# High and low part of the input in one product of 512 columns, both sums added at eviction

## The chip, the cores and the metric

The kernel runs on one core of a Trainium2 chip. The metric is the device time of one execution in microseconds, the median of several runs. TensorE (PE) multiplies, PEld is its weight load, VectorE is DVE, ScalarE is ACT, GpSimd is POOL, SyncE is SP. TensorE's clock is granted at one of two levels, 1.2 and 2.4 GHz; the profile gives it as a share of the higher.

## What is computed

Two transformer blocks, one behind the other, on 256 tokens of width 2048, all in fp32. Cut to the parts around the change:

```python
# first block, feed-forward (FFN_HIDDEN = 5632)
h = rms_norm(x, ln_ffn_pre)
u = causal_depthwise_conv(h @ w_ffn_up, ffn_conv_w, ffn_conv_b)     # 2048 -> 2 * 5632, 3 taps
gate, up = jnp.split(u, [FFN_HIDDEN], axis=-1)
f = (gelu_tanh(gate) * up) @ w_ffn_down                             # 5632 -> 2048
x = x + rms_norm(f, ln_ffn_post)

# second block, after its mixer: peer_ffn, 8 heads, 16 experts of 16384 for each head and token
q = (hf @ w_pq).reshape(T, 8, 2, 128)                               # routing queries
s = einsum('thpc,hpnc->thpn', q, sub_keys)                          # then top 16 of 128, twice, and of their sums
act = gelu(einsum('cd,ckd->ck', h, take(u_tab, experts))) * gate    # first table
out = einsum('ck,ckd->cd', act, take(v_tab, experts))               # second table
```

Ahead of the feed-forward the first block has an attention and a state-space mixer, and the second block has a recurrent mixer and an attention ahead of its experts.

## The kernel before

**Precision by two parts.** Every large product is made in the type fp32r from a high and a low part: for weights w = hi + lo and input x = xh + xl the kernel sums hi·xh, hi·xl and lo·xh in PSUM. The input's parts are made once (`k.hh`, `k.hl`, each 128 x 16 blocks x 256 tokens; in the feed-forward's second product `gh`, `gl`, 44 blocks). The weights' parts are made as they stream in: `_stream` (L232 on) loads `raw` from memory on SP's queue, ScalarE copies it to `hi` (L252), VectorE makes `lo = raw - hi` (L255). In the first block a chunk of hi and lo is 1024 columns (four blocks of 128 input rows by 256 output columns) with three buffers, in the second 512 columns (two blocks) with four.

**A step.** `_proj` takes the blocks of one group of 256 output columns: for each block and each half of 128 output columns it issues three matmuls of 256 columns (tokens), each with weights of its own, into one PSUM bank `acc`. A step over 16 blocks is 16 x 2 x 3 = 96 matmuls, one over 44 blocks 264. The weights are the stationary side, the input is the moving side. All matmuls are recorded at L260.

**Feed-forward** (`_ffn`, L684). 44 steps over `w_up`, the first three of them held open together and fed in parts (`_lead`, `LEAD2`) while the input's blocks arrive. Behind each step VectorE multiplies `acc` by the token's factor into `u` (L700), does the three taps of the convolution (L704, L707), ScalarE the gelu (L709), and the result is split into `gh` and `gl` (L710 to L712). Then eight steps over `w_dn`, each evicted by ScalarE (squares, L633 and L636) and VectorE (scaling, L626).

**Routing and first table** (`_peer`, L1485 on; `_Route.head`, L1353). 64 steps over the first table `u`; before every third of the first 24 a head is computed: a step over `w_pq`, its eviction to `pq` (L1359), eight small products with the sub-keys into `ps_sk`, then the top values on VectorE. Step i of the table gives two columns of experts for all tokens. Up to step 27 (`done == 0`) it is evicted straight to its place (L1568) and put through the gelu. From step 27 on `spread` builds two tokens' selection from one-hot products (`ps_g`), which ScalarE and VectorE take out of PSUM (L1542, L1543), and the steps from 28 are evicted to `gtmp` (L1573). `acc` has three buffers of one bank in all these places; PSUM has eight banks.

**Second table.** Products of 512 columns into `o` (hi·ah, lo·ah, hi·al), each with weights of its own, beside gathered rows from memory.

The order of instructions on each engine comes from a planner that simulates the kernel's timeline with estimated durations and priorities; each engine then works its list in order.

## Time and profile before

| | |
|---|---|
| median of three runs | 3312.84 us (3309.78 to 3317.23) |
| the profiled execution's own time | 3315.16 us |
| its span, first to last instruction | 3313.4 us |
| mean granted TensorE clock | 0.989 |
| matmuls | 24762 |
| busy: PE, PEld, DVE, ACT, POOL | 97%, 91%, 77%, 49%, 33% of the span |

A row's duration on PE runs from a matmul's start to its modelled end and overlaps the next ones, so matmuls are priced by the distance between starts. "Idle before" is the time in which the engine stood still ahead of an instruction, with what ended it. A row of the windows view gives the stretch and its length, then for each engine the busy time and in brackets the instructions that touch the stretch.

### The profile page before, as it was taken

Reading aid. Unit: us, or ns where it says so; the run is one execution under the profiler, and the core shown is the slowest. Engines: PE = TensorE matmul, PEld = TensorE weight load, DVE = VectorE, ACT = ScalarE, POOL = GpSimd, SP = SyncE. Lnnn points to the kernel's source line nnn. Section 1 sums busy time; section 2 is a strip of 40 time slices with the busy share of each in tenths; the row PEclk is TensorE's granted clock in tenths of the full one; section 3 lists DMA queues with packets and bytes.
Section 4 is the critical chain, followed back from the end, with each engine's and each line's share of the span. In section 5 each row is a group of like instructions: output and inputs, shape, how many; then the busy total and the mean of one; then the engine's idle time right before and its main releaser. Section 6 shows DMA issues by size and latency. Waiting matters only on the chain.

```text
span 3313.4 us, 66459 instructions
## 1 busy us (share of the span) xinstructions
PE 3217.2 (97%) x24762; PEld 3024.0 (91%) x24762; DVE 2556.5 (77%) x6016; ACT 1614.8 (49%) x3131; POOL 1079.8 (33%) x1266
## 2 busy tenths in 40 slices
PE   8999999999999989999999899999999999999998
PEld 8999899999999979888868899999999997777776
DVE  8775587777754468788875587877999997898998
ACT  4444354444433345455554544445556554555554
POOL 2110100000000034444430000003889976666663
PEclk9999999999999989999999999999999999999999
DMA  5445445555555546543417776666666669999996
GB/s 198 160 162 172 151 159 179 186 183 182 187 179 185 182 158 223 157 144 122 127 44 251 245 226 201 194 194 202 191 183 197 187 196 339 353 344 347 346 346 234
DMA packets 240372, 680.50 MB, mean 205 GB/s; under 512 B 59184, under 2 KB 89776, under 8 KB 215856
## 3 DMA queue, kind: packets, MB, share of 16 engines
q1 hardware_dynamic: 168848, 560.53, 51.9%
q0 software_dynamic: 20480, 83.90, 7.1%
q10 hardware_dynamic: 50720, 31.82, 3.3%
q8 instruction: 194, 3.18, 0.4%
q14 instruction: 130, 1.06, 0.1%
HBM read 649.55 MB, written 60.16 MB: 214 GB/s over the span
## 4 chain that ended last, share of the span: by engine, by line
PE 83%; DVE 8%; DMA 5%; ACT 2%; issue 1%; POOL 1%; ACTq 0%; SPq 0%; DVEq 0%
PE acc L260 57%; PE o L260 15%; PE held L260 3%; DVE lo L255 2%; DMA raw<-in_w_out 1%; PE R L260 1%; PE ps_g L260 1%; ACT hi L252 1%; DVE hl L350 1%; PE ps_S L260 1%; DVE ltmp L1040 1%; DMA x3n<-nat 1%; PE ps_p L260 0%; DMA dst<-s 0%; PE ps_sc L260 0%
## 5 line engine op out<-in xcount | busy, mean ns | idle before, releaser
L252 ACT ACTIVATE hi<-raw 128x512 fp32r<-128x512 f32 (+1 forms) x1582 | 1145.3, 731 | 1223.3 <-PE acc L260 740.6
L255 DVE TENSOR_TENSOR lo<-raw,hi 128x512 fp32r<-128x512 f32 (+1 forms) x1492 | 1227.5, 835 | 555.8 <-ACT hi L252 550.8
L260 PE MATMUL acc<-hh,hi 128*128 128x256 f32 x4928 | 1401.4, 285 | 13.0 <-ACT hh L349 11.6
L260 PE MATMUL acc<-hh,lo 128*128 128x256 f32 x4928 | 1401.9, 285 | 11.4 <-DVE lo L255 10.4
L260 PE MATMUL acc<-hl,hi 128*128 128x256 f32 x4928 | 1399.0, 284 | 6.1 <-DVE hl L350 5.9
L260 PEld LDWEIGHTS acc<-hh,hi 128*128 128x128 f32 x4928 | 934.8, 190 | 16.5 <-ACT hh L349 12.3
L260 PEld LDWEIGHTS acc<-hh,lo 128*128 128x128 f32 x4928 | 931.3, 189 | 16.8 <-DVE lo L255 13.3
L260 PEld LDWEIGHTS acc<-hl,hi 128*128 128x128 f32 x4928 | 936.6, 190 | 9.7 <-DVE hl L350 8.5
L260 PE MATMUL o<-lo,ah 128*128 128x512 f32 x768 | 305.0, 397 | 2.1 <-DVE lo L255 2.0
L260 PE MATMUL o<-hi,al 128*128 128x512 f32 x768 | 303.8, 396 | 0.0
L1456 POOL DMA_INDIRECT vrow<-wide,prow x256 | 261.1, 1020 | 66.7 <-issue 40.8
L1525 POOL TENSOR_SCALAR oh<-iota,sel 128x128 fp32r<-128x128 f32 x256 | 203.0, 803 | 93.2 <-PE ps_g L260 79.7
L260 PE MATMUL o<-hi,ah 128*128 128x512 f32 x768 | 221.9, 398 | 8.5 <-ACT hi L252 7.6
L699 POOL MEMSET u<- 128x4 f32 x44 | 4.5, 103 | 653.5 <-DVE y L707 510.3
L260 PE MATMUL acc<-gh,lo 128*128 128x256 f32 x704 | 199.2, 283 | 0.0
L260 PE MATMUL acc<-gl,hi 128*128 128x256 f32 x704 | 199.2, 283 | 0.0
L260 PE MATMUL acc<-gh,hi 128*128 128x256 f32 x704 | 199.2, 283 | 0.0
L255 POOL TENSOR_TENSOR lo<-raw,hi 128x512 fp32r<-128x512 f32 (+1 forms) x90 | 133.3, 1482 | 166.1 <-ACT hi L252 156.0
L260 PEld LDWEIGHTS o<-hi,ah 128*128 128x128 f32 x768 | 143.2, 188 | 48.2 <-ACT hi L252 13.5
L260 PEld LDWEIGHTS o<-lo,ah 128*128 128x128 f32 x768 | 144.5, 188 | 40.0 <-DVE lo L255 5.1
L1478 DVE SCALAR_TENSOR_TENSOR o<-vrow,pval,o 128x512 f32<-128x512 f32 x254 | 179.0, 750 | 0.0
L260 PEld LDWEIGHTS o<-hi,al 128*128 128x128 f32 x768 | 144.6, 188 | 35.0 <-POOL al L1603 0.2
(480 smaller groups left out, 4675.5 us busy)
## 6 DMA issues: line engine op xcount, KB each, us to landing
raw<-in_u SPq DMA_DIRECT2D x256, 512.0 KB, 4.6
raw<-in_w_up SPq DMA_DIRECT2D x85, 1024.0 KB, 5.2
raw<-in_v SPq DMA_DIRECT2D x128, 512.0 KB, 6.3
raw<-in_w_in SPq DMA_DIRECT2D x43, 1024.0 KB, 5.2
raw<-in_w_dn SPq DMA_DIRECT2D x40, 1024.0 KB, 4.8
wide<-in_vs SPq DMA_DIRECT2D x128, 256.0 KB, 4.8
raw<-in_v SPq DMA_DIRECT2D x128, 256.0 KB, 6.0
raw<-in_w_rkv SPq DMA_DIRECT2D x48, 512.0 KB, 3.9
```

Source lines behind the costliest of these rows:

```text
L252: nc.scalar.activation(hi[:, :m], raw[:, a:a + m], AF.Copy)
L255: k.low = eng.tensor_tensor(lo[:, :m], raw[:, a:a + m], hi[:, :m].bitcast(F32), op=OP.subtract)
L260: return k.nc.tensor.matmul(out, lhsT, rhs, start=start, stop=stop, skip_group_check=True)
L350: k.nc.vector.scalar_tensor_tensor(lo, t, scale, hi.bitcast(F32), op0=OP.mult, op1=OP.subtract)
L699: nc.gpsimd.memset(u[:, :, 0:2], 0.0)
L1040: nc.vector.tensor_tensor(tmp[:, :, 0:t], tt[:, :, 0:t], lq[:, 0:t, t][:, None, :].to_broadcast([128, 8, t]), op=OP.mult)
L1456: nc.gpsimd.indirect_dma_start(r, None, wide, bass.IndirectOffsetOnAxis(ap=picks.row[:, t, j:j + 1], axis=0), element_offset=128 * t)
L1478: i = nc.vector.scalar_tensor_tensor(acc[t], v, w, acc[t], op0=OP.mult, op1=OP.add)
L1525: nc.gpsimd.tensor_scalar(a[:, j], iota, sel[:, 0, t:t + 1], None, op0=OP.is_equal)
```

## The change

A new helper `_proj2` does a step with two matmuls for each block and half instead of three: hi times [xh | xl], 512 columns into a whole bank, and lo times xh, 256 columns added to the bank's first half. So a step's result has two banks, one for each half of the output columns. `_sum2` takes it out: ScalarE copies the second halves of both banks (the sum of hi·xl) to SBUF, VectorE adds the first halves. For this the input's two parts lie side by side in one tile (`hx`, `gx`). It is used in all 44 steps over `w_up`, in seven of the eight over `w_dn`, in the eight heads and in table steps 0 to 27; the other steps keep `_proj` and write the first bank of their two. `acc` has three such tiles in the feed-forward (with two instead of three for `psw`) and two in routing and tables.

```diff
@@ -260,6 +260,27 @@
     return k.nc.tensor.matmul(out, lhsT, rhs, start=start, stop=stop, skip_group_check=True)
 
 
+def _proj2(k, ps, w, kts, x, first=True, last=True):
+    k0, k1 = kts
+    kt = k0
+    for hi, lo, m in _stream(k, w[:, k0 * 256:k1 * 256], (k1 - k0) * 256):
+        for a in range(0, m, 256):
+            for c in range(2):
+                cs = slice(a + c * 128, a + c * 128 + 128)
+                _mm(k, ps[:, c].rearrange("p n t -> p (n t)"), hi[:, cs], x[:, kt].rearrange("p n t -> p (n t)"),
+                    start=first and kt == k0)
+                _mm(k, ps[:, c, 0], lo[:, cs], x[:, kt, 0], stop=last and kt == k1 - 1)
+            kt += 1
+def _sum2(k, out, ps):
+    k.nc.scalar.activation(out, ps[:, :, 1], AF.Copy)
+    k.nc.vector.tensor_tensor(out, ps[:, :, 0], out, op=OP.add)
 def _proj(k, ps, w, kts, xh, xl, first=True, last=True, natural=False):
 
     k0, k1 = kts
@@ -287,12 +308,16 @@
             kt += 1
 
 
-def _lead(k, w, prs, parts, name="acc"):
-
-    held = [k.acc.tile([128, 2, 256], F32, name=name) for _ in prs]
+def _lead(k, w, prs, parts, name="acc", both=False):
+    held = [k.acc.tile([128, 2, 2, 256] if both else [128, 2, 256], F32, name=name) for _ in prs]
     for n, part in enumerate(parts):
         for ps, pr in zip(held, prs):
-            _proj(k, ps, w[pr], part, k.hh, k.hl, first=n == 0, last=n == len(parts) - 1)
+            ends = dict(first=n == 0, last=n == len(parts) - 1)
+            if both:
+                _proj2(k, ps, w[pr], part, k.hx, **ends)
+            else:
+                _proj(k, ps, w[pr], part, k.hh, k.hl, **ends)
     return held
 
 
@@ -684,20 +709,22 @@
 def _ffn(k, I, c2, sqa):
     nc, tc = k.nc, k.tc
     g1 = c2.enter_context(tc.tile_pool(name="g1", bufs=1))
-    gh = g1.tile([128, 44, 256], F32R, name="gh")
-    gl = g1.tile([128, 44, 256], F32R, name="gl")
+    gx = g1.tile([128, 44, 2, 256], F32R, name="gx")
+    gh, gl = gx[:, :, 0], gx[:, :, 1]
     _, rb = _token_rstd(k, [sqa[:, 0], sqa[:, 1]], D, g1, "c")
     with tc.tile_pool(name="g2", bufs=2) as g2:
-        lead = _lead(k, I["w_up"], range(3), LEAD2)
+        lead = _lead(k, I["w_up"], range(3), LEAD2, both=True)
         for j in range(44):
             if j < 3:
                 ps = lead[j]
             else:
-                ps = k.acc.tile([128, 2, 256], F32, name="acc")
-                _proj(k, ps, I["w_up"][j], (0, KT), k.hh, k.hl)
+                ps = k.acc.tile([128, 2, 2, 256], F32, name="acc")
+                _proj2(k, ps, I["w_up"][j], (0, KT), k.hx)
+            z = g2.tile([128, 2, 256], F32, name="z")
+            _sum2(k, z, ps)
             u = g2.tile([128, 2, 258], F32, name="u")
             nc.gpsimd.memset(u[:, :, 0:2], 0.0)
-            nc.vector.tensor_tensor(u[:, :, 2:258], ps, _bc2(rb), op=OP.mult)
+            nc.vector.tensor_tensor(u[:, :, 2:258], z, _bc2(rb), op=OP.mult)
             y = g2.tile([128, 2, 256], F32, name="y")
             for n in range(2):
                 t = j + 44 * n
@@ -714,10 +741,16 @@
         f = g3.tile([128, KT, 256], F32, name="f2")
         sqs = [sqa]
         for pr in range(8):
-            ps = k.acc.tile([128, 2, 256], F32, name="acc")
-            _proj(k, ps, I["w_dn"][pr], (0, 44), gh, gl)
-            _sq_acc(k, g3, sqs, ps, pr)
-            _scaled(k, f, ps, "ln_ffn_post", pr)
+            ps = k.acc.tile([128, 2, 2, 256], F32, name="acc")
+            if pr < 7:
+                z = f[:, pr * 2:pr * 2 + 2]
+                _proj2(k, ps, I["w_dn"][pr], (0, 44), gx)
+                _sum2(k, z, ps)
+            else:
+                z = ps[:, 0]
+                _proj(k, z, I["w_dn"][pr], (0, 44), gh, gl)
+            _sq_acc(k, g3, sqs, z, pr)
+            _scaled(k, f, z, "ln_ffn_post", pr)
         _, rb = _token_rstd(k, _sq_list(sqs), D, g3, "d")
         _residual(k, g4, f, rb, "norm1", sqa)
 
@@ -1353,10 +1386,11 @@
     def head(self, h):
         k, p2 = self.k, self.p2
         nc = k.nc
-        ps = k.acc.tile([128, 2, 256], F32, name="acc")
-        _proj(k, ps, self.I["w_pq"][h], (0, KT), k.hh, k.hl)
+        ps = k.acc.tile([128, 2, 2, 256], F32, name="acc")
+        _proj2(k, ps, self.I["w_pq"][h], (0, KT), k.hx)
         q = p2.tile([128, 2, 256], F32, name="pq")
-        nc.vector.tensor_tensor(q, ps, _bc2(self.rb), op=OP.mult)
+        _sum2(k, q, ps)
+        nc.vector.tensor_tensor(q, q, _bc2(self.rb), op=OP.mult)
         sp = k.psw.tile([128, 2, 2, 128], F32, name="ps_sk", tag="psw")
         i0 = None
         for t in range(2):
@@ -1506,7 +1540,7 @@
 
     with ExitStack() as sctx:
         with ExitStack() as c:
-            k.acc = c.enter_context(tc.tile_pool(name="accp", bufs=3, space=bass.MemoryType.PSUM, side="right"))
+            k.acc = c.enter_context(tc.tile_pool(name="accp", bufs=2, space=bass.MemoryType.PSUM, side="right"))
             k.psw = c.enter_context(tc.tile_pool(name="pswp", bufs=4, space=bass.MemoryType.PSUM))
             t2 = tctx.enter_context(tc.tile_pool(name="rt2", bufs=2))
             route = _Route(k, I, rb, t1, t2)
@@ -1561,16 +1595,18 @@
                     gate = g1.tile([128, 256], F32, name="gate")
                     nc.scalar.activation(gate.bitcast(F32R), sel[:, 2], AF.Copy)
                     nc.vector.tensor_tensor(sel[:, 2], sel[:, 2], gate, op=OP.subtract)
-                ps = k.acc.tile([128, 2, 256], F32, name="acc")
-                _proj(k, ps, I["u"][i], (0, KT), k.hh, k.hl)
+                ps = k.acc.tile([128, 2, 2, 256], F32, name="acc")
                 dst = next(parts(2 * i, 2 * i + 2))[0]
                 if done == 0:
-                    nc.vector.tensor_tensor(dst, ps, _bc2(rb), op=OP.mult)
+                    _proj2(k, ps, I["u"][i], (0, KT), k.hx)
+                    _sum2(k, dst, ps)
+                    nc.vector.tensor_tensor(dst, dst, _bc2(rb), op=OP.mult)
                     nc.scalar.activation(dst, dst, AF.Gelu)
                     keep(dst, i, 0, 256)
                 else:
+                    _proj(k, ps[:, 0], I["u"][i], (0, KT), k.hh, k.hl)
                     tmp = g1.tile([128, 2, 256], F32, name="gtmp")
-                    nc.vector.tensor_tensor(tmp, ps, _bc2(rb), op=OP.mult)
+                    nc.vector.tensor_tensor(tmp, ps[:, 0], _bc2(rb), op=OP.mult)
                     nc.scalar.activation(tmp[:, :, :done], tmp[:, :, :done], AF.Gelu)
                     keep(tmp, i, 0, done)
                     if done < 256:
@@ -1649,8 +1685,8 @@
 def _first_block(k, I, xp, sqa):
     nc, tc = k.nc, k.tc
     with ExitStack() as c1:
-        k.psw = c1.enter_context(tc.tile_pool(name="psw", bufs=3, space=bass.MemoryType.PSUM))
         with ExitStack() as c2:
+            k.psw = c2.enter_context(tc.tile_pool(name="psw", bufs=3, space=bass.MemoryType.PSUM))
             mp = c2.enter_context(tc.tile_pool(name="mix", bufs=1))
             mh = mp.tile([128, KT, 256], F32R, name="mh")
             ml = mp.tile([128, KT, 256], F32R, name="ml")
@@ -1675,6 +1711,7 @@
             with tc.tile_pool(name="rsd", bufs=3) as rp:
                 _residual(k, rp, f, rb, "ln_ffn_pre", sqa)
         with ExitStack() as c2:
+            k.psw = c2.enter_context(tc.tile_pool(name="pswf", bufs=2, space=bass.MemoryType.PSUM))
             k.acc = c2.enter_context(tc.tile_pool(name="accf", bufs=3, space=bass.MemoryType.PSUM))
             _ffn(k, I, c2, sqa)
 
@@ -1761,8 +1798,8 @@
     nc.vector.memset(k.ones, 1.0)
     hctx, cctx = ExitStack(), ExitStack()
     hp = hctx.enter_context(tc.tile_pool(name="h", bufs=1, side="right"))
-    k.hh = hp.tile([128, KT, 256], F32R, name="hh")
-    k.hl = hp.tile([128, KT, 256], F32R, name="hl")
+    k.hx = hp.tile([128, KT, 2, 256], F32R, name="hx")
+    k.hh, k.hl = k.hx[:, :, 0], k.hx[:, :, 1]
     cp = cctx.enter_context(tc.tile_pool(name="cols", bufs=1, side="right"))
     k.cols = cp.tile([128, I["cols"].shape[1]], F32, name="cols")
     sqa = cp.tile([128, 2, 256], F32, name="sqa")
```

## Rows read from the trace of the kernel before

**Rows 1.** The page: busy time, granted clock, chain that ended last

```profile
PE 3217.2 (97%) x24762; PEld 3024.0 (91%) x24762; DVE 2556.5 (77%) x6016; ACT 1614.8 (49%) x3131; POOL 1079.8 (33%) x1266
...
PEclk9999999999999989999999999999999999999999
...
PE 83%; DVE 8%; DMA 5%; ACT 2%; issue 1%; POOL 1%; ACTq 0%; SPq 0%; DVEq 0%
PE acc L260 57%; PE o L260 15%; PE held L260 3%; DVE lo L255 2%; DMA raw<-in_w_out 1%; PE R L260 1%; PE ps_g L260 1%; ACT hi L252 1%; DVE hl L350 1%; PE ps_S L260 1%; DVE ltmp L1040 1%; DMA x3n<-nat 1%; PE ps_p L260 0%; DMA dst<-s 0%; PE ps_sc L260 0%
```

**Rows 2.** Windows: busy of PE, PEld, DVE, ACT, POOL; clock, DMA share, GB/s

```profile
400.00:450.00 50.00, 40.16 (x298) 38.75 (x297) 38.78 (x86) 24.18 (x45) 0.00 (x0) 0.86 0.41 137
500.00:900.00 400.00, 400.00 (x3336) 400.00 (x3335) 292.09 (x453) 172.29 (x208) 3.50 (x34) 1.00 0.56 184
950.00:1150.00 200.00, 200.00 (x1669) 200.00 (x1668) 88.97 (x81) 76.67 (x76) 9.24 (x5) 1.00 0.54 185
1200.00:1700.00 500.00, 471.80 (x4347) 427.07 (x4347) 411.85 (x1136) 256.36 (x628) 237.70 (x327) 0.97 0.47 146
1850.00:1905.00 55.00, 47.16 (x357) 44.84 (x356) 33.40 (x63) 30.46 (x58) 8.22 (x6) 0.94 0.69 216
1910.00:2240.00 330.00, 330.00 (x2757) 330.00 (x2756) 264.33 (x753) 157.24 (x255) 0.00 (x0) 1.00 0.65 203
2300.00:2700.00 400.00, 398.38 (x3328) 397.97 (x3327) 382.50 (x1225) 237.26 (x673) 346.85 (x386) 1.00 0.65 190
2750.00:3250.00 500.00, 491.03 (x2079) 389.38 (x2078) 448.14 (x1066) 252.65 (x463) 341.64 (x363) 1.00 0.97 349
```

**Rows 3.** The page's costliest groups: busy us, mean ns, idle before

```profile
L260 PE MATMUL acc<-gh,hi 128*128 128x256 f32 x704 | 199.2, 283 | 0.0
```

**Rows 4.** Timeline of DVE: start, us, instruction, idle before; two table evictions

```profile
2273.97 0.69 DVE L1568 TENSOR_TENSOR sa<-acc,rs_bcp 128x512 f32<-128x512 f32 x1 [0.20 <-PE acc L260]
...
2285.49 0.69 DVE L1568 TENSOR_TENSOR sb<-acc,rs_bcp 128x512 f32<-128x512 f32 x1 [0.16 <-PE acc L260]
```

**Rows 5.** Windows of tile o alone: PE, PEld, DVE; clock, DMA share

```profile
2900.00:2950.00 50.00, 50.00 (x215) 40.20 (x214) 16.93 (x24) 1.00 0.96 336
```

**Rows 6.** Timeline of PE: products with w_dt's 16-column weights

```profile
58.82 0.28 PE L260 MATMUL ps_dt<-hh,wdh 128*16 128x256 f32 x1
...
59.95 0.28 PE L260 MATMUL ps_dt<-hl,wdh 128*16 128x256 f32 x1
```

**Rows 7.** Groups by form: squares (950:1150), u (500:900), selection out of PSUM (2300:2700)

```profile
L636 ACT ACTIVATE sqp<-acc 128x512 f32<-128x512 f32 x5 | 2.9, 582 | 0.0
...
L700 DVE TENSOR_TENSOR u<-acc,rs_bcc 128x512 f32<-128x512 f32 x35 | 24.2, 692 | 21.9 <-PE acc L260 21.9
...
L1542 ACT ACTIVATE gsum<-ps_g 128x104 f32<-128x104 f32 x122 | 30.6, 251 | 18.7 <-DVE sa L1545 11.9 <-DVE sb L1545 2.1 <-DVE sb L1543 1.4
L1543 DVE TENSOR_TENSOR gsum<-ps_g,gsum 128x104 f32<-128x104 f32 x121 | 30.5, 253 | 0.0
```

**Rows 8.** Timeline of ACT and DVE at a step's boundary of the first product

```profile
700.05 1.06 ACT L252 ACTIVATE hi<-raw 128x1024 fp32r<-128x1024 f32 x1 [1.81 <-PE acc L260]
...
700.86 0.73 DVE L704 TENSOR_SCALAR y<-u,cols 128x256 f32<-128x256 f32 x2
701.50 1.22 DVE L255 TENSOR_TENSOR lo<-raw,hi 128x1024 fp32r<-128x1024 f32 x1
702.64 0.48 DVE L707 SCALAR_TENSOR_TENSOR y<-u,cols,y 128x256 f32<-128x256 f32 x1
```

**Rows 9.** Timeline of DVE and PE: a head's query and its products

```profile
2025.96 0.69 DVE L1359 TENSOR_TENSOR pq<-acc,rs_bcp 128x512 f32<-128x512 f32 x1 [0.20 <-PE acc L260]
...
2029.01 0.50 PE L260 MATMUL ps_sk<-sk,pq 128*128 128x128 f32 x3
```

**Rows 10.** Timeline of PE and DVE: a late step's last matmul, its eviction

```profile
2707.35 0.28 PE L260 MATMUL acc<-hh,lo 128*128 128x256 f32 x1
...
2714.90 0.68 DVE L1573 TENSOR_TENSOR gtmp<-acc,rs_bcp 128x512 f32<-128x512 f32 x1
```

## Prediction

> **What bounds the kernel now.** I read the page first. TensorE is busy for 97% of the span at full clock nearly throughout, and the chain of work that ended last is 83% TensorE, 57% of it products into the tile acc [rows 1]. A high busy share alone doesn't prove a bound, since matmuls overlap, so I cut the span into stages with the windows view [rows 2]. In the feed-forward's first product (500 to 900 us), its second (950 to 1150), the routing with the early table steps (1910 to 2240) and the late table steps (2300 to 2700) TensorE has no idle time to speak of, while VectorE is at 73%, 44%, 80% and 96%, ScalarE at 38% to 59% and the DMA engines at 54% to 66%. So in the first three of these, which the change touches, time is the number of matmuls times their pitch. Two short stretches are different: the start of the feed-forward (400 to 450 us, TensorE 40.2 of 50 and a mean granted clock of 0.86, thus partly at the lower of its two levels) and the start of the routing (1850 to 1905, 47.2 of 55). There the matmuls wait for their inputs.
>
> **The pitch now.** The duration of a matmul row (283 ns, [rows 3]) overlaps its neighbours and is no price. The price is start to start. In the window from 950 to 1150 us 1669 matmuls of 256 columns touch 200 us; about two lie in it only partly, so 200 / 1667 = 120.0 ns. Two evictions of neighbouring early table steps confirm it: 2285.49 - 2273.97 = 11.52 us for 96 matmuls, again 120.0 ns [rows 4].
>
> **The change, part by part.** (1) For each block of 128 input rows and 128 output columns (a "pair" of old and new form below) three matmuls of 256 columns, each with its weight load, become one of 512 and one of 256. The columns streamed stay 768; what goes is one matmul and one weight load. What a 512-column product of the same types costs is shown by the second table's products into o: 215 touch 50 us without idle time, each lasts about 0.39 us, so 1.7 lie in it only partly and 50 / 213.3 = 234.4 ns [rows 5]. I take this value, since the row has the same types, the same 128-column weights, a load for each product and no wait. A pair then goes from 3 x 120.0 = 360.0 to 234.4 + 120.0 = 354.4 ns, a gain of 5.6 ns; the bounds, 226.7 and 240 ns for the 512 columns, are the first two rivals below. What that gain consists of is seen from w_dt's products: 256 columns with weights of only 16 columns go at (59.95 - 58.82) / 10 = 113 ns [rows 6]. A full weight load thus seems to cost about 7 ns a product, and the rest grows with the columns: 2 x 113 + 7 = 233, near the 234.4 seen.
>
> How many pairs: first product 44 x 16 x 2 = 1408; second, seven of eight, 7 x 44 x 2 = 616; queries 8 x 16 x 2 = 256; table steps 0 to 27 (the code's done is still zero there) 28 x 16 x 2 = 896. Sum 3176. From these I take off the 96 pairs of the feed-forward's three held tiles and 96 at the start of the routing, where the input sets the pace [rows 2]; 3080 - 96 = 2984 remain, times 5.6 ns = **16.7 us** less. (With all of them, 17.8.)
>
> (2) The eviction grows. Each of 44 + 7 + 8 + 28 = 87 steps gets a ScalarE copy of 128x512 out of PSUM (0.582 us by the nearest row, the squares out of acc) and a VectorE add with one side in PSUM (0.692 us, like u's eviction) [rows 7]. That is 51 us of ScalarE and 60 us of VectorE in all; in the first product VectorE goes from 73% to 79%, at most 86% in the early table steps. I cost it at nothing: the matmuls of the next step write another acc tile meanwhile, and a step lasts 11.5 us against 1.3 us more eviction. If that cover were gone everywhere, it would cost 87 x 1.27 = 111 us; a gain isn't possible, as nothing is removed from these engines. What waits behind it: on ScalarE the next high-part copy, on VectorE the next low part. At a step's boundary near 700 us the copy for three chunks ahead starts at 700.05 and its low part ends at 702.72; two chunks of 24 matmuls (5.8 us) are ready before it is wanted, near 705.8 [rows 8]. So 3.1 us of cover stand against 1.3.
>
> (3) In the eight heads TensorE's products with the sub-keys wait for the query. The query is there at 2026.65 and they start at 2029.01, 2.36 us later [rows 9], so 1.27 us more costs nothing; without the cover it would be 8 x 1.27 = 10 us.
>
> (4) acc in routing and table steps has two buffers instead of three, each of two banks. With two, step n+2 waits for the eviction of step n. In the late steps, where VectorE is fullest, the latest eviction I found starts at 2714.90, 7.5 us after its step's last matmul at 2707.35, and the next step lasts over 11.5 us [rows 10]. About 4 us of cover are left: nothing. If it were gone, each late microsecond would be one of TensorE.
>
> (5) Both parts of the input in one tile, psw opened with two buffers for the feed-forward, the first 512-column product wanting the low part one matmul earlier: 0.12 us once at each start, no more. The last of the second product's steps keeps the old form, so the path into the norm behind it is the old one. No DMA is added or moved; the loads of later weights only come as early as TensorE frees their buffers, at 54% to 66% DMA share.
>
> (6) The order on each engine is planned from estimated times, so stages with idle gaps (1200 to 1700 us, TensorE 471.8 of 500 [rows 2]) may come out a little differently though their code is the same. I bound this at 5 us either way, about a sixth of these gaps.
>
> **Sum.** The profiled execution took 3315.16 us (span 3313.4), 2.3 above the median of 3312.84. 3315.2 - 16.7 = 3298.5 for it, and on the median 3312.8 - 16.7 = **3296 us**, 0.5% faster; its own range by (6) and the excluded pairs is 3289 to 3306.
>
> **Rivals.** *A fixed cost for each matmul.* At the granted 2.4 GHz 256 columns take 106.7 ns, so 13.3 ns of the 120.0 are something else. If that is fixed, 512 columns take 213.3 + 13.3 = 226.7, the pair gains 13.3 ns and the time is 3312.8 - 39.7 = 3273. For it: the one place with 512 columns is also the one where DMA engines are at 97% [rows 2], which might slow it there. Against it: the 234.4 itself. The Trainium skill (TensorE: Matmul & The Clock Gate, section Back-to-back issue gap) goes further this way: the gap is columns / 2.4 plus about 2.5 ns, 215.8 for 512. By that the pair would gain 24.2 ns and the time be some 3241; the trace's 234.4 disagrees.
>
> *The load was hidden, and columns alone count.* Then 512 cost 2 x 120.0, nothing is gained, and the time is 3313, the same. For it: the loads lie beside the matmuls in time. Against it: 113 against 120 ns for light and full loads [rows 6] and 234.4 under 240 [rows 5]. The Trainium skill (same page, section Step-by-step: what each phase is for) speaks for this rival: the next weights load from a port of their own while a matmul runs, so that one load fewer frees nothing. That no such load costs anything is what rows 6 contradict.
>
> *The eviction as one block ahead of the low parts.* This is the slower side, in the first product's 44 boundaries. If VectorE ran the add and the multiplication (0.69 each), the two scalings (0.73) and the eight operations on 128x256 that follow there and on ScalarE (0.48 each, priced like the conv step of [rows 8]), behind ScalarE's copy (0.58), and only then the next low part (1.22), that would end 7.75 us after 700.05. It is wanted after 5.75: a wait of 2.0 us a step, 44 x 2.0 = 88 us, time 3384. It decides from 16.7 / 44 = 0.38 us a step. Against it: before, the low part is put between the scalings and the conv steps [rows 8], and the late steps have the same pair of copy and add out of PSUM, 122 times in 400 us [rows 7], with VectorE at 96% and TensorE 1.6 us idle [rows 2].
>
> **How the numbers follow.** Forecast 70%, fixed cost 8%, hidden load 14%, block 8%. A measurement of this kernel can tell about 0.2% (6.6 us) from no change. Faster by that: 70 + 8 - 1 for the forecast's upper edge = 77%; same 14%; slower 9%, the block and that 1%. The range goes from 3270, the fixed cost, to 3312, which takes in the forecast and nearly half of the hidden load: together over 8 in 10.
>
> **What would show it.** Right: 24762 - 3176 = 21586 matmuls; pairs at about 354 ns start to start in the first product (an early table step of 11.34 us in place of 11.52); first and second product shorter by some 7.4 and 3.4 us; no TensorE idle time on hi, lo or the copy; the stages from 1200 to 1700 us as long as before. Wrong: 512-column matmuls at 227 or under (fixed cost) or at 240 (hidden load); idle time of TensorE ended by lo or hi at each boundary (block); waits of the late steps' first matmul on gtmp's eviction (two buffers).

## The result, and the profile after

The changed kernel takes 3286.99 us (median; 3281.25 to 3292.42) against 3313.45 us (3309.78 to 3321.03) for the kernel before beside it: a ratio of 0.992, with a 95% interval of 0.9907 to 0.9933. That is 26.5 us less. The profiled execution's span is 3288.6 us against 3313.4 before, with a granted clock of 0.988. TensorE, with 21586 matmuls (the counts at the end of each entry), is as full as before [rows 1]:

```profile
PE 3183.3 (97%) x21586; PEld 2849.4 (87%) x21586; DVE 2607.8 (79%) x6103; ACT 1658.6 (50%) x3218; POOL 1083.2 (33%) x1266
...
PE 83%; DVE 8%; DMA 4%; ACT 2%; issue 2%; POOL 1%; ACTq 0%; DVEq 0%; SPq 0%; POOLq 0%
```

The windows of the same stages, to be held against [rows 2]; each window lies inside its stage (columns: stretch, length, then busy time and instructions of PE, PEld, DVE, ACT, POOL, then clock, DMA share, GB/s):

```profile
500.00:900.00 400.00, 400.00 (x2287) 348.89 (x2286) 325.67 (x504) 194.68 (x250) 3.72 (x36) 1.00 0.57 188
950.00:1120.00 170.00, 170.00 (x983) 149.91 (x982) 87.43 (x80) 71.42 (x75) 9.05 (x5) 1.00 0.56 191
1200.00:1690.00 490.00, 460.25 (x4258) 414.99 (x4259) 395.44 (x1111) 245.41 (x606) 228.03 (x323) 0.98 0.48 146
1930.00:2200.00 270.00, 270.00 (x1561) 236.09 (x1560) 227.93 (x622) 143.26 (x237) 0.00 (x0) 1.00 0.67 202
2300.00:2690.00 390.00, 387.19 (x3225) 386.13 (x3224) 373.54 (x1200) 230.58 (x654) 344.09 (x375) 1.00 0.65 190
```

The three changed stages still show no idle time of TensorE. In the first, 2287 matmuls touch 400 us. With two of them only partly inside, that is 1142.5 pairs of 350.1 ns. In the second, (983 - 2) / 2 = 490.5 pairs in 170 us are 346.6 ns each. Before it was 360.0 in both. The late steps, whose code is as before, stay near theirs (3225 matmuls in 390 us against 3328 in 400).

TensorE's timeline shows what a pair consists of: first two stretches of the first product, then the second product.

```profile
599.88 0.39 PE L260 MATMUL acc<-hx,hi 128*128 128x512 f32 x1
600.11 0.28 PE L260 MATMUL acc<-hx,lo 128*128 128x256 f32 x1
600.23 0.39 PE L260 MATMUL acc<-hx,hi 128*128 128x512 f32 x1
600.47 0.28 PE L260 MATMUL acc<-hx,lo 128*128 128x256 f32 x1
...
999.90 0.39 PE L260 MATMUL acc<-gx,hi 128*128 128x512 f32 x1
1000.13 0.28 PE L260 MATMUL acc<-gx,lo 128*128 128x256 f32 x1
1000.25 0.39 PE L260 MATMUL acc<-gx,hi 128*128 128x512 f32 x1
```

From 599.88 to 600.23 and from 999.90 to 1000.25 it is 0.35 us. A start-to-start mean over the pairs of the first product's window gives 232.1 ns behind the 512 columns and 117.9 behind the 256, 350.0 together. In the second product's window it gives 230.0 + 116.7 = 346.7. The early table steps give 232.4 + 118.2 = 350.6, and the products into o 234.3.

**Where the 24.8 us between the two spans went.** The marks are starts of instructions in the two timelines.

| stretch | before, us | after, us | difference |
|---|---|---|---|
| start to the feed-forward's first product | 415.1 | 421.9 | +6.8 |
| first product | 515.2 | 500.7 | -14.5 |
| second product | 253.3 | 245.1 | -8.2 |
| mixer and attention, to the routing's first product | 668.7 | 668.3 | -0.4 |
| routing's first product to the first late eviction | 457.0 | 447.9 | -9.1 |
| late steps | 433.9 | 433.0 | -0.8 |
| second table and the end | 570.2 | 571.7 | +1.5 |

The marks of the second product and of the late steps stand in the lists by tile (shortest, mean and longest ns, then the first and the last start). The second line runs from the first late eviction, 2283.9; before, it was at 2309.3:

```profile
L260 PE MATMUL acc<-gx,lo x704: 280/280/285, 922.8 to 1167.7; 128*128 128x256 f32 x176
...
L1609 DVE TENSOR_TENSOR gtmp<-acc,rs_bcp x36: 669/675/692, 2283.9 to 2717.3; 128x512 f32<-128x512 f32 x36
```

The routing's first product, first in the kernel before, then in the changed one:

```profile
1852.28 0.28 PE L260 MATMUL acc<-hh,hi 128*128 128x256 f32 x1
```

```profile
1835.98 0.39 PE L260 MATMUL acc<-hx,hi 128*128 128x512 f32 x1
```

The second head's products with the sub-keys are no good mark here: with the new form twelve more pairs run ahead of them than before.

The 6.8 us at the start have two parts. The last product of the attention's output into held starts at 409.56 instead of 405.08, 4.5 us later. Up to there the kernel's code is the same; the chain of waits differs in its first long piece, the landing of a piece of the input. First the kernel before, then the changed one:

```profile
4.90 6.58 DMA x<-in_x
```

```profile
5.52 8.44 DMA x<-in_x
```

It was there at 11.48 and at 13.96. The same piece landed between 12.8 and 13.9 us in further profiles of changed kernels, and the output's end lay between 404.6 and 410.8. These 4.5 us are thus mostly scatter of single executions, though both profiles of the old form lie at the early edge (the kernel before, and below with its weights moved: 11.5 and 12.2 us, 405.1 and 404.7). The other 2.3 us belong to the change. First the kernel before, then the changed one:

```profile
415.10 1.01 PE L260 MATMUL acc<-hh,hi 128*128 128x256 f32 x3 [2.79 <-ACT hh L349]
417.09 0.58 PE L260 MATMUL acc<-hl,hi 128*128 128x256 f32 x1 [0.99 <-DVE hl L350]
```

```profile
415.83 1.19 PE L260 MATMUL ps_bc<-ident,rs_yb 128*128 128x128 f32 x4 [2.83 <-DVE rs_yb L335]
421.90 0.76 PE L260 MATMUL acc<-hx,hi 128*128 128x512 f32 x1 [4.88 <-DVE hx L375]
```

Before, three products of the three held tiles needed only the high part and ran at 415.10, and TensorE then waited for the low part until 417.09. Now already the first product wants both parts and waits for VectorE's hx. From the end of the attention's output to the first product it is 12.3 us instead of 10.0. Some of this is made up at once: from the output's end to the 200th pair, less 200 pairs at their pitch, it is 20.2 us instead of 18.4, so the start costs 1.8 us.

**The eviction** cost what it was priced at. The add and the copy, from 500 to 900 us (busy us, mean ns, idle before); no TensorE time is lost on them:

```profile
L281 DVE TENSOR_TENSOR z<-acc,z 128x512 f32<-128x512 f32 x36 | 24.6, 682 | 0.0
L280 ACT ACTIVATE z<-acc 128x512 f32<-128x512 f32 x35 | 20.4, 582 | 0.0
```

### The profile page after: what moved, and what is told of

It is laid out like the page before. It is cut to its first block, busy times and chain, and to the rows that moved or that the text cites. A ratio compares the mean times of both kernels' runs of the same rounds, so it can differ in the third digit from the quotient of the medians.

```text
span 3288.6 us, 60301 instructions
## 1 busy us (share of the span) xinstructions
PE 3183.3 (97%) x21586; PEld 2849.4 (87%) x21586; DVE 2607.8 (79%) x6103; ACT 1658.6 (50%) x3218; POOL 1083.2 (33%) x1266
## 4 chain that ended last, share of the span: by engine, by line
PE 83%; DVE 8%; DMA 4%; ACT 2%; issue 2%; POOL 1%; ACTq 0%; DVEq 0%; SPq 0%; POOLq 0%
PE acc L260 55%; PE o L260 16%; PE held L260 5%; DVE lo L255 1%; PE R L260 1%; PE ps_g L260 1%; ACT hi L252 1%; DVE ltmp L1073 1%; DMA wide<-sb 1%; DVE hx L375 1%; DMA s<-g 1%; PE ps_p L260 1%; PE ps_sc L260 1%; DMA x3n<-nat 0%; DMA dst<-s 0%
## 5 line engine op out<-in xcount | busy, mean ns | idle before, releaser
L260 PE MATMUL acc<-hx,hi 128*128 128x256 f32 (+1 forms) x7296 | 1802.5, 325 | 24.3 <-ACT hx L374 11.8
L260 PE MATMUL acc<-hx,lo 128*128 128x256 f32 x4928 | 1393.2, 284 | 12.8 <-DVE lo L255 12.3
L260 PEld LDWEIGHTS acc<-hx,hi 128*128 128x128 f32 x7296 | 1226.6, 190 | 142.5 <-ACT hx L374 12.3
L260 PEld LDWEIGHTS acc<-hx,lo 128*128 128x128 f32 x4928 | 932.8, 189 | 22.2 <-DVE lo L255 17.3
L260 PE MATMUL acc<-gx,hi 128*128 128x512 f32 (+1 forms) x792 | 245.3, 367 | 0.0
L1559 POOL TENSOR_SCALAR oh<-iota,sel 128x128 fp32r<-128x128 f32 x256 | 206.1, 816 | 84.0 <-PE ps_g L260 64.8
L260 PE MATMUL acc<-gx,lo 128*128 128x256 f32 x704 | 197.4, 280 | 0.0
L260 PEld LDWEIGHTS o<-hi,ah 128*128 128x128 f32 x768 | 143.4, 189 | 48.6 <-ACT hi L252 13.9
L260 PEld LDWEIGHTS acc<-gx,hi 128*128 128x128 f32 x792 | 142.6, 188 | 25.3
L1562 POOL TENSOR_SCALAR oh<-iota,sel 128x128 fp32r<-128x128 f32 x128 | 150.8, 1178 | 1.1 <-DVE sel L1597 1.1
L663 POOL TENSOR_TENSOR sqa<-sqa,sqp 128x512 f32<-128x512 f32 x18 | 29.8, 1656 | 326.2 <-ACT sqp L661 326.2
```

The source lines that it names most:

```text
L260: return k.nc.tensor.matmul(out, lhsT, rhs, start=start, stop=stop, skip_group_check=True)
L663: nc.gpsimd.tensor_tensor(sqs[0], sqs[0], sq, op=OP.add)
L1559: nc.gpsimd.tensor_scalar(a[:, j], iota, sel[:, 0, t:t + 1], None, op0=OP.is_equal)
L1562: eng.tensor_scalar(b[:, j, n], iota, sel[:, 1, t:t + 1], w[:, t:t + 1], op0=OP.is_equal, op1=OP.mult)
```

## The experiments

The pairs gained 10.0, 13.3 and 9.4 ns instead of 5.6, in one kernel with one code for the pair. What tells hx's pairs from gx's? The two theories: a product costs its columns and a fixed 13.3 ns, and something at hx and in o adds to that; or a full weight load costs 7 ns, as the prediction had it. A place to look for that something is where the operands lie. In the kernel's own addresses hi begins in each partition at byte 33920 in the feed-forward and at 29824 in the second block, gx at 74880 and hx at 196576. So gx stands a multiple of 512 bytes above hi, and hx a multiple of 512 and 352 bytes more (lo stands a multiple of 512 above hi, which changes nothing in this). In the second table ah stands above hi by a multiple of 512 and 352 too. Below, a time without a bracket behind it is of one execution, and there only stages are compared.

**The input's tile moved by 32 bytes.**

```diff
     k.hx = hp.tile([128, KT, 2, 256], F32R, name="hx")
+    hp.tile([128, 8], F32, name="hpad")
```

> The changed kernel with a tile of 32 bytes behind hx in its pool, so that hx begins at byte 196544 of a partition (a multiple of 64) instead of 196576. Nothing else moves in the second table stage. Theory F (a product with its weight load costs columns / 2.4 GHz + 13.3 ns; hx's place, 32 bytes off a multiple of 64, adds 3 to 4 ns a pair): pairs of the feed-forward's first product go from 350.0 to 346.7 ns, those of heads and early table steps from 351 to 346.7, about 9 us less in all; the second product (gx, already on a multiple of 64) stays at 346.7, the products into o at 234.3. Theory M (the gain comes from 512 and 256 columns taking turns, place does not matter): every pitch as in the changed kernel, time the same.

It took 3283.85 us. The distance from hi to hx is now 320 beyond a multiple of 512. The place does matter, but not in the way of a 64-byte boundary: the first product's pairs got longer, and the late steps, with 256 columns only, got shorter. The windows of the first product and of the late steps:

```profile
500.00:900.00 400.00, 400.00 (x2267) 348.32 (x2266) 322.23 (x496) 193.15 (x249) 3.71 (x36) 1.00 0.57 187
...
2300.00:2690.00 390.00, 386.78 (x3267) 384.57 (x3267) 375.72 (x1202) 231.83 (x661) 350.52 (x376) 1.00 0.67 192
```

The first is 1132.5 pairs of 353.2 ns instead of 350.1, and the second 3267 instead of 3225 matmuls. Start to start, the 256 columns of the late steps went at 117.9 ns instead of 120.1, and the late steps took 427.0 instead of 433.0 us. The second product stayed at 346.7 and o at 234.4. The early table steps, with the same pair and the same distance as the first product, moved much less, to 351.7 ns:

```profile
1930.00:2200.00 270.00, 270.00 (x1556) 236.35 (x1555) 227.51 (x622) 142.98 (x236) 0.00 (x0) 1.00 0.67 203
```

**The whole right side moved by 32 bytes**, the second table's ah and al with it.

```diff
     nc.vector.memset(k.ones, 1.0)
+    tp = ctx.enter_context(tc.tile_pool(name="top", bufs=1, side="right"))
+    tp.tile([128, 8], F32, name="tpad")
```

> The changed kernel with 32 bytes kept free at the upper end of the memory for the whole run, so that hx and also ah and al (the second table's stationary side) begin on multiples of 64. Theory F: as with hx alone (some 9 us less), and the products into o go from 234.3 to 226.7 ns; with 2304 of them that is up to 17.5 us more, as far as the DMA engines, at 97% there, allow: 9 to 27 us less than the changed kernel. Theory M: no change anywhere.

It took 3275.65 us (3271.19 to 3279.40), a ratio of 0.9885 [0.9869, 0.9902] to the kernel before. The first product's pairs took 353.4 ns, the late steps 425.9 us (117.4 ns a product), the products into o 233.5 instead of 234.3. So o follows the place of ah, a little.

**The low part of the weights times both parts of the input**, so that every product of the new form has 512 columns.

```diff
-                _mm(k, ps[:, c, 0], lo[:, cs], x[:, kt, 0], stop=last and kt == k1 - 1)
+                _mm(k, ps[:, c].rearrange("p n t -> p (n t)"), lo[:, cs], x[:, kt].rearrange("p n t -> p (n t)"),
+                    stop=last and kt == k1 - 1)
```

> The changed kernel with lo multiplied by both parts too, so that every pair is two products of 512 columns (it adds the product of the two low parts, leaves nothing out). Theory F: a pair of the second feed-forward product costs 2 x 226.7 = 453.3 ns, of the first 2 x (226.7 + 3.3) = 460 at most; some 340 us more in all. Theory M (512 next to 512 goes at the 234.4 ns of o): 468.8 ns everywhere, some 375 us more.

It took 3641.8 us, as much more work would. What counts is the pitch. The timeline of PE in the second product:

```profile
1199.80 0.39 PE L260 MATMUL acc<-gx,hi 128*128 128x512 f32 x1
1200.03 0.39 PE L260 MATMUL acc<-gx,lo 128*128 128x512 f32 x1
1200.26 0.39 PE L260 MATMUL acc<-gx,hi 128*128 128x512 f32 x1
...
1201.16 0.39 PE L260 MATMUL acc<-gx,hi 128*128 128x512 f32 x1
```

From 1199.80 to 1201.16 it is six products, 0.227 us each; the mean over the stage's products of 512 columns is 226.7 ns. That is 512 / 2.4 = 213.3 and 13.3 more, while 256 columns take 106.7 and 13.3 more, 120.0. With hx in the first product, the same form takes 233.3, 6.6 ns more; in o 234.5. So 512 columns can go at 226.7 with a full load each, and the 234.4 of [rows 5] holds 7.7 ns that are neither the columns' nor this fixed cost.

**The eviction done twice.**

```diff
     k.nc.scalar.activation(out, ps[:, :, 1], AF.Copy)
+    k.nc.scalar.activation(out, ps[:, :, 1], AF.Copy)
     k.nc.vector.tensor_tensor(out, ps[:, :, 0], out, op=OP.add)
+    k.nc.vector.tensor_tensor(out, out, out, op=OP.max)
```

> The changed kernel with the eviction's added work doubled: ScalarE copies the second sum twice, VectorE follows its add with a maximum of the result with itself. If the eviction lies beside the matmuls, as forecast: the same time as the changed kernel within some 5 us, and TensorE as full as there. If it stands on the path: up to 87 x (0.58 + 0.69) = 111 us more; the part of it that shows is the part that the change pays already.

It took 3288.43 us. The first product lasted 500.4 us (500.7), the second 245.1 (245.1). The window of the first product has as many matmuls as without the second eviction (2288 against 2287), with VectorE at 346.5 us instead of 325.7:

```profile
500.00:900.00 400.00, 400.00 (x2288) 348.87 (x2287) 346.52 (x539) 208.26 (x287) 3.69 (x36) 1.00 0.57 189
```

In the feed-forward a second eviction costs nothing, and so the first one doesn't either. In the routing and the early table steps it is less sure: from the routing's first product to the first late eviction it took 450.6 us, against 447.9 in the changed kernel and 446.0 to 449.0 in the other runs of this form. The late steps, which don't have this eviction, took 437.4 us in this execution.

**The weights moved down by 160 bytes**, by a shorter tile ahead of them. Then hi to hx, hi to gx and hi to ah are all multiples of 512 bytes.

```diff
-    k.ones = res.tile([128, 128], F32, name="ones")
+    k.ones = res.tile([128, 88], F32, name="ones")
```

> The changed kernel with the tile ones 88 instead of 128 columns wide, which moves everything on the lower side of the memory, hi and lo among it, 160 bytes down: hx then begins a multiple of 512 bytes from the weights' chunks (196576 - 29664 = 326 x 512), as gx does (88 x 512) and as ah does, while hx itself stays at the place where the changed kernel has it. Theory R (what a pair costs over 346.7 ns depends on the distance of the moving from the stationary side, 0 at multiples of 512 bytes): pairs of the first feed-forward product, heads and early table steps at 346.7 ns, 8 to 9 us less than the changed kernel; late table steps at 120.0 ns a matmul; the products into o at 226.7 ns, up to 17 us less, as far as the DMA engines allow. Theory U (it is the upper end of the memory that costs, whatever the distance): pairs with hx at 350, o at 234, the same time.

It took 3266.6 us (3262.14 to 3279.28), a ratio of 0.9872 [0.9846, 0.9898] to the kernel before: the fastest of all. Its windows of the first product and of the second table, then o's list by tile:

```profile
500.00:900.00 400.00, 400.00 (x2309) 349.70 (x2308) 328.27 (x507) 197.09 (x253) 3.69 (x36) 1.00 0.58 190
...
2750.00:3230.00 480.00, 473.93 (x2076) 388.19 (x2077) 446.72 (x1073) 253.36 (x464) 322.60 (x348) 1.00 0.97 354
...
L260 PE MATMUL o<-hi,al x768: 388/389/796, 2706.4 to 3244.8; 128*128 128x512 f32 x192
```

In the first, (2309 - 2) / 2 pairs are 346.8 ns each, as with gx, and the first product lasts 495.9 instead of 500.7 us. The products into o go at 227.2 ns instead of 234.3, and all of them take 540.3 instead of 555.1 us, with the DMA engines as busy as before. The late steps took 429.7. But the early table steps, with the same pair and the same distance, stayed at 350.3 ns, with as many matmuls in their window as in the changed kernel; why is open.

```profile
1930.00:2200.00 270.00, 270.00 (x1561) 236.00 (x1560) 227.88 (x625) 143.34 (x236) 0.00 (x0) 1.00 0.67 202
```

**gx moved by 192 bytes** on top of that, the other way round: the stage that was at 346.7 should get worse.

```diff
     g1 = c2.enter_context(tc.tile_pool(name="g1", bufs=1))
+    g1.tile([128, 48], F32, name="gpad")
     gx = g1.tile([128, 44, 2, 256], F32R, name="gx")
```

> As the run before, and gx alone moved up by 192 bytes, so that its distance from the weights is no multiple of 512 any more. Theory R: the pairs of the second feed-forward product cost more than 346.7 ns, some 350 to 353, 2 to 4 us in all; the rest as in the run before. Theory U: they stay at 346.7.

It took 3276.7 us. The second product's window has 481 pairs of 353.4 ns in place of 490.5 of 346.6, and it lasted 248.6 instead of 245.1 us:

```profile
950.00:1120.00 170.00, 170.00 (x964) 147.66 (x963) 85.32 (x78) 69.81 (x73) 8.98 (x5) 1.00 0.55 187
```

The first product (496.0) and o (540.3) stayed; the late steps took 433.7 us against 429.7, with nothing of theirs moved, so that much is scatter of single executions there. The two feed-forward products and o each follow the distance between their own two operands, for better (hx, o) and for worse (hx, gx); the early table steps don't.

**Half of the low part's weights**, in the second product.

```diff
-def _proj2(k, ps, w, kts, x, first=True, last=True):
+def _proj2(k, ps, w, kts, x, first=True, last=True, half=128):
...
-                _mm(k, ps[:, c, 0], lo[:, cs], x[:, kt, 0], stop=last and kt == k1 - 1)
+                ls = slice(cs.start, cs.start + half)
+                _mm(k, ps[:half, c, 0], lo[:, ls], x[:, kt, 0], stop=last and kt == k1 - 1)
...
-                _proj2(k, ps, I["w_dn"][pr], (0, 44), gx)
+                _proj2(k, ps, I["w_dn"][pr], (0, 44), gx, half=64)
```

> The changed kernel, leaving out lo's product for the second 64 of each 128 output columns in seven of the eight steps over w_dn: the 256-column matmul there has weights of 64 columns. If the 13.3 ns of a product beside its columns are its weight load: less than 346.7 ns a pair, down to some 340 (the step that the forecast took from w_dt's 16-column weights, 113 instead of 120 ns). If they go with the product whatever it loads: 346.7 as in the changed kernel, and the same time.

It took 3282.63 us. Every second load has 64 columns instead of 128 and is shorter, as PEld's 124.9 us in the window against 149.9 show, and the matmuls are as many as in the changed kernel, 983:

```profile
950.00:1120.00 170.00, 170.00 (x983) 124.92 (x982) 86.64 (x80) 69.98 (x73) 9.01 (x5) 1.00 0.56 190
```

The second product lasted 245.1 us, as before the edit. From 64 to 128 columns of a load the cost doesn't grow here.

**The kernel before with its weights moved by 160 bytes.** The short tile of ones, alone in the kernel before.

> The kernel before with ones 88 instead of 128 columns wide, and nothing else: hi and lo 160 bytes lower, so that hh, hl and ah stand multiples of 512 bytes from the weights, as in the run with the changed kernel. It tells what that placing gives by itself. By what has been seen so far: pairs of three 256-column matmuls stay at 360.0 ns, both feed-forward products as long as before, the products into o at 227 in place of 234.4 ns, that is 14 to 15 us less in all, near 3299. If it also speeds up the 256-column pairs, the changed kernel's gain of 10 to 13 ns a pair would partly be the placing's: then the first feed-forward product, too, is shorter than before.

It took 3298.21 us (3297.10 to 3305.17), a ratio of 0.996 [0.9944, 0.9975]. The windows of the first product and of the second table:

```profile
500.00:900.00 400.00, 400.00 (x3336) 400.00 (x3335) 292.31 (x454) 172.42 (x208) 3.50 (x35) 1.00 0.55 184
...
2750.00:3250.00 500.00, 489.59 (x2128) 399.00 (x2127) 458.05 (x1096) 258.58 (x473) 351.71 (x374) 0.99 0.98 358
```

The first has the same 3336 matmuls as [rows 2]: three products of 256 columns gain nothing from the place. The second has 2128 against 2079, o at 227.2 ns and 540.8 instead of 553.9 us. So the place alone is worth some 15 us, all in the second table. And at this place the change is worth 3298.2 - 3266.6 = 31.6 us.

**The feed-forward alone in the new form**; heads and early table steps as before, with three accumulators of one bank.

```diff
-        ps = k.acc.tile([128, 2, 2, 256], F32, name="acc")
-        _proj2(k, ps, self.I["w_pq"][h], (0, KT), k.hx)
+        ps = k.acc.tile([128, 2, 256], F32, name="acc")
+        _proj(k, ps, self.I["w_pq"][h], (0, KT), k.hh, k.hl)
...
-            k.acc = c.enter_context(tc.tile_pool(name="accp", bufs=2, space=bass.MemoryType.PSUM, side="right"))
+            k.acc = c.enter_context(tc.tile_pool(name="accp", bufs=3, space=bass.MemoryType.PSUM, side="right"))
...
-                ps = k.acc.tile([128, 2, 2, 256], F32, name="acc")
+                ps = k.acc.tile([128, 2, 256], F32, name="acc")
+                _proj(k, ps, I["u"][i], (0, KT), k.hh, k.hl)
```

> The changed kernel with heads and early table steps undone (three matmuls a pair, one bank and three buffers for acc there). If the parts add up as the changed kernel's trace shows them: some 10 us more than the changed kernel, all of it between the second head and the first late step; the late steps, with three buffers again, as long as with two (433 us). If two buffers cost the late steps something, these come out shorter here.

It took 3289.75 us, only some 3 above the changed kernel. But this execution reached the feed-forward 4.1 us earlier, and its mixer and attention were 4.2 us shorter. The stages themselves: first product 500.5, second 245.1, the routing's first product to the first late eviction 456.9 against 447.9 (457.0 in the kernel before), late steps 433.2 against 433.0. The windows of the early and of the late steps:

```profile
1930.00:2200.00 270.00, 269.72 (x2251) 269.51 (x2250) 207.66 (x573) 127.41 (x207) 0.00 (x0) 1.00 0.64 196
2300.00:2690.00 390.00, 388.59 (x3244) 388.02 (x3243) 375.17 (x1200) 230.99 (x657) 347.23 (x379) 1.00 0.66 190
```

So the early part is worth about 9 us and the two-bank accumulators cost the late steps nothing that shows: with three, 433.2 us.

## Why the prediction was right, and which term was off

The sign, the mechanism and the range held: 26.5 us less against 16.7 forecast, 3287 against 3296. The narrower range that the forecast gave itself, 3289 to 3306, was missed by 2 us. That the time came out nearer to the forecast than to the 3273 of the fixed cost, which had 8%, is partly luck: the pairs alone gained 31.2 us, nearer to that rival's 39.7, and the late start of the feed-forward hid some of it. Step by step:

- **TensorE bounds the changed stages.** Right: no idle time there before or after, and an eviction of double length changes nothing in the feed-forward.
- **The count.** Right: 21586 matmuls.
- **Term (1), the pair, was mis-sized.** It put 5.6 ns on each of 2984 pairs. Measured: 10.0 in the first product (1312 pairs, 13.1 us), 13.3 in the second (616, 8.2 us), 9.4 in heads and early steps (1056, 9.9 us), together 31.2 in place of 16.7. The step that was off is the price of 512 columns, 234.4 ns from o [rows 5]. The prediction took it because the row had the same types, the same weights and no wait. It didn't ask where the two operands lie. With the weights moved by 160 bytes the same row is 227.2 ns, with the DMA engines no less busy, so the rival's guess that DMA slows o isn't it either. The bound that the prediction kept, 226.7, is the price at the good place, and the rival of a fixed cost had the mechanism for products that lie so: 13.3 ns a product whether it has 256 or 512 columns.
- **Seven ns for a full weight load.** Fell. Half of a load's columns away moved nothing. And the 113 ns of [rows 6] are a price of the place too: 46 steps between such products are 113.4 ns each in the kernel before, and with hx moved by 32 bytes (70.59 - 65.26) / 46 = 115.9. In that run 256 columns with full loads went at 117.0 ns in the first 410 us and at 117.9 in the late steps, so of the 7 ns some 1 to 2 are left there.

```profile
65.26 0.28 PE L260 MATMUL ps_dt<-hx,wdh 128*16 128x256 f32 x1
...
70.59 0.28 PE L260 MATMUL ps_dt<-hx,wdl 128*16 128x256 f32 x1
```

- **Term (2), the eviction at nothing.** Right in the feed-forward, with 0.582 and 0.682 us near the prices forecast (0.582 and 0.692); in the early steps a microsecond or two isn't excluded. The rival of a block ahead of the low parts found no place: TensorE doesn't wait.
- **Terms (3) and (4).** Right. A head's query still comes before its products want it, as the timelines of VectorE and TensorE show (compare [rows 9]); the two buffers cost the late steps nothing that shows.

```profile
2006.60 0.68 DVE L1393 TENSOR_TENSOR pq<-pq,rs_bcp 128x512 f32<-128x512 f32 x1
...
2010.82 1.05 PE L260 MATMUL ps_sk<-sk,pq 128*128 128x128 f32 x8
```

- **Term (5), 0.12 us for a start.** Too small for the feed-forward: there it is 2.3 us to the first product and 1.8 in the end. Before, three products ran while the low part was made, and now the first one waits.
- **Term (6), the planner.** Right: -0.4 us in the mixer and attention, whose code is the same. In the other runs this stretch took 663.2 to 670.1 us, so a difference of that size is scatter.
- **The sign by eviction distance**, 11.34 us for an early step, came out and means little. Two of them:

```profile
2258.22 0.68 DVE L281 TENSOR_TENSOR sb<-acc,sb 128x512 f32<-128x512 f32 x1
2269.59 0.68 DVE L281 TENSOR_TENSOR sb<-acc,sb 128x512 f32<-128x512 f32 x1
```

These are 11.37 us apart, but 32 pairs of 350.6 ns are 11.22, and a selection product stands in between. The window's count is the better sign.

The account closes: 31.2 us by the pairs, 0.6 more in the three stages' marks (31.8), 6.8 given back at the start, of which 2.3 belong to the change, and 0.3 elsewhere, make 24.7 of the 24.8 us between the spans.

Two rules of the Trainium skill stand beside this (TensorE: Matmul & The Clock Gate). The section Back-to-back issue gap of the Trainium skill gives columns / 2.4 and about 2.5 ns for a gap that it calls isolated, and for a stream of loads and matmuls about 131 ns at 512 columns. The trace has such a stream and agrees with neither: the form fits the products with gx, but with 13.3 ns in place of 2.5, 226.7 at 512 columns. The section Step-by-step: what each phase is for of the Trainium skill says that the next weights load through a port of their own and take no read bandwidth from the running matmul. The halved load agrees (346.7 ns a pair with either).

## What to carry to other kernels

Merge products that share their weights: every matmul saved gave 9 to 13 ns here, the columns being the same, and the longer eviction was free because the next step's matmuls covered it. A pitch read at another place of the kernel is a price only for operands that lie in the same way; when two stages with one code differ by a few ns a product, compare the addresses before looking for contention; that they don't explain every stage, the early table steps show. Moving one tile costs nothing, and it can be worth nearly as much as the edit itself: some 15 us in the kernel before, some 20 in the changed one.

## What the runs showed of the hardware

In the two feed-forward products, the late steps and o, the time from start to start depends on how far the moving operand lies from the stationary one, counted modulo 512 bytes (the higher address less the lower). All at a granted clock of 0.99 or 1.00, in ns:

| distance | pair (512 + 256) | 512 after 512 | 256 after 256 |
|---|---|---|---|
| 0 | 346.7 (gx; hx with weights moved) | 226.7 (gx), 227.2 (o with weights moved) | 120.0 (kernel before with weights moved) |
| 352 | 350.0 (hx) | 233.3 (hx), 234.3 (o) | 120.0 (kernel before), 120.1 (late steps) |
| 320 | 353.3 (hx moved by 32) | 233.5 (o, right side moved) | 117.4, 117.9 (late steps) |
| 192 | 353.3 (gx moved by 192) | | |

What the runs show is the dependence and its size, not its cause. 512 as the modulus is a reading that all of the table fits; other distances were not run in these stages. Three things don't fit it, and it isn't settled why. The early table steps hardly follow the distance (350.6 at 352, 351.7 at 320, 350.3 at 0). The products with w_dt's 16-column weights, which lie 64 bytes further on from block to block, go at 113.4 ns at all multiples of 64 and at 115.9 where the distance is 32 beyond one. And in the first block's products with the weights as the moving side, 256 columns go at 118.0 ns at 352, 115.0 at 320 and 119.5 at 0. Nor is it settled whether the fixed 13.3 ns belong to the product or to having a load at all, since no run had a product without its own load. That 256 columns alone are fastest at 320, where the pair is slowest, was not expected and stays unexplained.
